# Feed-forward output projection of two layers: seven quarter products for each pair of groups in place of eight

## The chip, the cores and the metric

The kernel runs on one core of one Trainium2 chip. The metric is the device time of one execution in microseconds; the median of three runs of the kernel before is 1320.17 us (1319.09 to 1320.4). The engines are TensorE (PE: matmuls, and PEld: its weight loads), VectorE (DVE), ScalarE (ACT), GpSimd (POOL) and SyncE (SP, which issues the transfers). SBUF is the on-chip memory that all of them read; PSUM, in eight banks of 128 x 512 words, is where TensorE writes its sums, and is called a bank here.

## The reference

Two decoder layers on 512 tokens of width 1024. Each layer has an attention part, a residual sum and a normalization, and then the part that the change is in, a feed-forward of width 2816:

```python
g, u = jnp.split(x @ w_gu, 2, axis=-1)
ffn = (jax.nn.silu(g) * u) @ w_down
ple = (p_i @ w_pp) * jax.nn.sigmoid(x @ w_pg)
return layer_norm(DN_ALPHA * x + ffn + ple, ln2_g, ln2_b)
```

All numbers are float32. `w_gu` is 1024 x 5632, `w_down` 2816 x 1024.

## The kernel before

TensorE multiplies rounded numbers, so each float32 operand is kept as a high part (a cast) and a low part (the operand less its high part), and each product is three matmuls: high x high, high x low, low x high (`mm3`, lines 253 to 256). The residual rows x0 to x3 are four tiles of 128 tokens by 1024.

**Weights** pass through one queue in the order in which they are used. A tile of up to 128 x 1024 words is loaded by SyncE into one of three buffers `wst` (L209), cast by ScalarE into the high half of one of five buffers `wsp` (L234), and GpSimd subtracts to make the low half (L235, "a split" in what follows). A `wsp` buffer comes free when TensorE has done its last matmul with it; that lets the cast of the tile five places on begin.

**The feed-forward** runs over 11 groups of 256 columns in each layer. `gate_up` makes a group: four weight tiles, 96 matmuls of 512 columns, then for each half of the group (the even and the odd 128 columns) a Silu (L793), a product on VectorE (L794, which reads a bank), a cast on ScalarE (L796) and a subtraction on VectorE (L797, both of whose inputs are in SBUF). The result is the transposed activation, 128 features by 512 tokens, in two parts. `GROUPS` cuts the 11 groups in two: after groups 0 to 5, and after 6 to 10, the output projection is made for all of them. For each half of the 1024 output columns four banks (one for each 128 tokens) take up the products with all the groups' weights, 24 matmuls for a group and column half, and only then `res_out` adds each bank to its residual rows (L715 the first time, where the residual is scaled, L713 after that). So there are 16 such additions in a layer.

**The layer's start.** The rows are normalized one tile after the other on VectorE (L340 and L342, on 128 x 1024 words, all inputs in SBUF; small steps L290 to L298 between them), TensorE transposes them (L350), and ScalarE and VectorE make the two parts (L352, L353). `gate_up` of group 0 does the tokens of x0 and x1 first, then needs x2 and x3.

The order of each engine's instructions is made when the program is built, by a scheduler; the functions below set the dependences and the buffers.

Of the kernel before, what the change touches and what calls it, by code (L numbers as in the profile page):

```python
# [26 lines left out]
FF = 2816  # L27
# [60 lines left out]
def hybrid_kernel(ctx: ExitStack, tc: tile.TileContext, x, p, positions, ln_in_g, ln_in_b, w_in,  # L88
# [83 lines left out]
    GROUPS = ((0, 6), (6, FF // 256))  # L172
    for l in range(L):
        for k, a in ((0, 3), (3, 3), (6, 2)):
            plan(a, rows(w_in[l], k, a, QI, NIN))
        for k in range(0, KT, 2):
            plan(2, rows(w_in[l], k, 2, KA, KA + 256), rows(w_in[l], k, 2, KB, KB + 128))
        for c in (QA, QA + 256, QB, QB + 256):
            for k in range(0, KT, 4):
                plan(4, rows(w_in[l], k, 4, c, c + 256))  # L180
        for k0 in (0, 4):
            for h in range(2):
                for k in range(k0, k0 + 4, 2):
                    plan(2, rows(w_o[l], k, 2, h * 512, (h + 1) * 512))
        for lo, hi in GROUPS:
            for f in range(lo, hi):
# [3 lines left out]
            for h in range(2):  # L190
                for f in range(lo, hi):
                    plan(2, rows(w_down[l], 2 * f, 2, h * 512, (h + 1) * 512))
# [9 lines left out]

    def w_pump():
        while True:
            go = False
            if wpos["dma"] < len(wq) and wpos["dma"] < wpos["split"] + ST_AHEAD:
                a, cols, _ = wq[wpos["dma"]]
                n = sum(ap.shape[1] for ap in cols)
                st = wst.tile([128, 1024], F32, name="wst", tag="wst")  # L209
                sv = st[:, :a * n].rearrange("p (a n) -> p a n", a=a)  # L210
                o = 0
                for ap in cols:
                    SP.dma_start(sv[:, :, o:o + ap.shape[1]], ap.rearrange("(a p) n -> p a n", p=128))
                    o += ap.shape[1]
                wst_live[wpos["dma"]] = st
                if wpos["dma"] in X_AT:
                    load_x(X_AT[wpos["dma"]])
                wpos["dma"] += 1
                go = True
            if wpos["split"] < wpos["dma"] and (wpos["room"] or wq[wpos["split"]][2]):  # L220
                i = wpos["split"]
                a, cols, extra = wq[i]
                n = sum(ap.shape[1] for ap in cols)
                st = wst_live.pop(i)
                if extra:
                    w = [[slot()[:, :n] for _ in range(a)] for _ in range(2)]
                    for k in range(a):
                        A.copy(w[0][k], st[:, k * n:(k + 1) * n])
                        V.tensor_tensor(w[1][k], st[:, k * n:(k + 1) * n], w[0][k], OP.subtract)
                    w_live[i] = w  # L230
                else:
                    wpos["room"] -= 1
                    w = wsp.tile([128, 2, 1024], F32R, name="wsp", tag="wsp")
                    A.copy(w[:, 0, :a * n], st[:, :a * n])  # L234
                    G.tensor_tensor(w[:, 1, :a * n], st[:, :a * n], w[:, 0, :a * n], OP.subtract)  # L235
                    w = w[:, :, :a * n].rearrange("p s (a n) -> p s a n", a=a)
                    w_live[i] = [[w[:, r, k] for k in range(a)] for r in range(2)]
# [5 lines left out]
    def w_take():  # L243
        i = wpos["use"]
        wpos["use"] += 1
# [7 lines left out]
    def mm3(o, sh, sl, mh, ml, start, stop):  # L253
        PE.matmul(o, sh, mh, start=start, stop=False)  # L254
        PE.matmul(o, sh, ml, start=False, stop=False)  # L255
        PE.matmul(o, sl, mh, start=False, stop=stop)  # L256
# [192 lines left out]
    for l in range(L):  # L449
# [319 lines left out]
        def gate_up(first):  # L769
# [5 lines left out]
            for r in ((0, 256), (256, 512)) if first else ((0, 512),):  # L775
                for j in range(2):
# [14 lines left out]
            for f in range(2):  # L791
                a, b = t2k(), t2k()
                A.activation(a, ps[0, f], AF.Silu)  # L793
                V.tensor_tensor(b, ps[1, f], a, OP.mult)  # L794
                h = [slot(), slot()]
                A.copy(h[0], b)  # L796
                V.tensor_tensor(h[1], b, h[0], OP.subtract)  # L797
                hs.append(h)
            return hs

        for gi, (lo, hi) in enumerate(GROUPS):
            hs = []
            for f in range(lo, hi):
                hs += gate_up(f == 0)
                if gi == 1 and f == lo:
# [9 lines left out]
            if gi == 0:  # L815
                pin = [slot(F32), slot(F32)]
                for i in range(2):
                    SP.dma_start(pin[i].rearrange("p (t n) -> p t n", t=2),
                                 p[l, 0, i * 256:(i + 1) * 256].rearrange("(t p) n -> p t n", p=128))
            for h in range(2):  # L820
# [10 lines left out]
                for t in range(NT):  # L831
                    res_out(h, ALPHA if gi == 0 else None)(t, ps[t])
# [68 lines left out]
```

## Time and profile before

| | |
|---|---|
| median of the runs | 1320.17 us (1319.09 to 1320.4) |
| the profiled execution | 1320.5 us |
| its span, from first to last instruction | 1318.7 us |
| TensorE busy, share of the span | 1271.0 us, 96% |
| VectorE busy | 613.8 us, 47% |
| GpSimd busy | 565.1 us, 43% |
| ScalarE busy | 511.7 us, 39% |
| mean granted TensorE clock | 0.985 of full speed |

The profiled execution's own time is 1.8 us more than its span. A busy share says how long an engine had work, not whether it held up the others; that is read from the idle times of the engine that is busy nearly always, and from what ended them. A matmul's row shows some 0.39 us, but they overlap: what one costs is the distance between two starts.

### The profile page before, as it was taken

To read this page: it belongs to the slowest core of one execution; us is meant where nothing else is said; L and a number is where in the kernel's file an instruction comes from. 1 tells how busy PE (TensorE), PEld (TensorE's weight loads), DVE (VectorE), ACT (ScalarE), POOL (GpSimd) and SP (SyncE) were. 2 spreads that over 40 slices of the span, in tenths; PEclk is the share of its full clock that TensorE was granted. 3 is DMA by queue.
4 is the path that set the end of the run, shared out by engine and by line. 5 is a ranking of instruction groups with operands and counts; after the bars stand their busy time and mean duration, and the time that the engine had idled before them with its cause. 6 is when DMAs were issued, how large, how long until landed. Compare 5 with 4: busy or idle time off the path is not lost.

```text
span 1318.7 us, 17770 instructions
## 1 busy us (share of the span) xinstructions
PE 1271.0 (96%) x6752; PEld 1097.1 (83%) x6752; DVE 613.8 (47%) x1522; ACT 511.7 (39%) x1056; POOL 565.1 (43%) x377
## 2 busy tenths in 40 slices
PE   6799999999999999999997999999999999999996
PEld 5799889888888888888897998979888888888885
DVE  8899965712120022113679998674121102121166
ACT  2657765333221232313336577743222212222220
POOL 7465432354444444443055544324444444444422
PEclk9899999899999999999998999999999999999998
DMA  5133011333333333324022301104332333332221
GB/s 168 49 96 97 33 33 33 97 105 99 98 113 97 96 96 97 96 96 138 12 80 81 113 33 49 48 17 144 96 96 96 112 96 96 96 96 96 96 80 48
DMA packets 88476, 112.72 MB, mean 85 GB/s; under 512 B 4804, under 2 KB 65220, under 8 KB 88392
## 3 DMA queue, kind: packets, MB, share of 16 engines
q1 hardware_dynamic: 87720, 111.57, 27.1%
q8 instruction: 53, 0.87, 0.3%
q14 instruction: 31, 0.25, 0.1%
q10 hardware_dynamic: 672, 0.03, 0.0%
HBM read 109.49 MB, written 2.10 MB: 85 GB/s over the span
## 4 chain that ended last, share of the span: by engine, by line
PE 84%; DVE 12%; ACT 2%; issue 1%; DMA 0%; POOL 0%; DVEq 0%; SPq 0%; POOLq 0%; ACTq 0%
PE bank L254 26%; PE bank L256 26%; PE bank L255 26%; PE bank L594 2%; PE bank L638 2%; DVE t2k L414 2%; DVE m L569 1%; DVE work L570 1%; DVE t2k L412 1%; PE bank L632 1%; DVE t2k L597 1%; DVE x L342 1%; DVE work L558 1%; PE bank L424 1%; PE bank L350 1%
## 5 line engine op out<-in xcount | busy, mean ns | idle before, releaser
L235 POOL TENSOR_TENSOR wsp<-wst,wsp 128x1024 fp32r<-128x1024 f32 (+3 forms) x188 | 448.9, 2392 | 527.6 <-ACT wsp L234 527.3
L234 ACT CAST wsp<-wst 128x1024 fp32r<-128x1024 f32 (+3 forms) x188 | 194.3, 1037 | 453.7 <-PE bank L256 286.5
L255 PE MATMUL bank<-fl,wsp 128*128 128x512 f32 (+1 forms) x768 | 286.1, 373 | 1.8 <-DVE fl L353 1.8
L256 PE MATMUL bank<-fh,wsp 128*128 128x512 f32 (+1 forms) x768 | 285.9, 373 | 0.0
L254 PE MATMUL bank<-fh,wsp 128*128 128x512 f32 (+1 forms) x768 | 284.9, 374 | 1.0 <-ACT fh L352 1.0
L794 DVE TENSOR_TENSOR t2k<-bank,t2k 128x512 f32<-128x512 f32 x44 | 30.0, 692 | 356.5 <-PE bank L256 356.5
L254 PE MATMUL bank<-wsp,slot 128*128 128x512 f32 x432 | 169.0, 391 | 0.0
L255 PEld LDWEIGHTS bank<-fl,wsp 128*128 128x128 f32 x768 | 145.9, 190 | 27.3 <-DVE fl L353 2.3
L256 PE MATMUL bank<-wsp,slot 128*128 128x512 f32 x432 | 168.2, 389 | 0.0
L255 PE MATMUL bank<-wsp,slot 128*128 128x512 f32 x432 | 168.2, 389 | 0.0
L254 PE MATMUL bank<-wsp,fh 128*128 128x256 f32 (+3 forms) x512 | 166.1, 326 | 1.3 <-DVE work L558 0.4
L254 PEld LDWEIGHTS bank<-fh,wsp 128*128 128x128 f32 x768 | 144.8, 190 | 26.6 <-ACT fh L352 1.9
L256 PEld LDWEIGHTS bank<-fh,wsp 128*128 128x128 f32 x768 | 145.8, 190 | 24.9
L256 PE MATMUL bank<-wsp,fl 128*128 128x256 f32 (+3 forms) x512 | 165.0, 323 | 1.5 <-DVE fl L353 1.5
L255 PE MATMUL bank<-wsp,fh 128*128 128x256 f32 (+3 forms) x512 | 164.5, 322 | 0.0
L254 PEld LDWEIGHTS bank<-wsp,fh 128*128 128x128 f32 x512 | 98.3, 192 | 7.7 <-ACT fh L352 1.0
L256 PEld LDWEIGHTS bank<-wsp,fl 128*128 128x128 f32 x512 | 98.2, 192 | 7.0 <-DVE fl L353 2.1
L255 PEld LDWEIGHTS bank<-wsp,fh 128*128 128x128 f32 x512 | 98.6, 193 | 5.5
L256 PEld LDWEIGHTS bank<-wsp,slot 128*128 128x128 f32 x432 | 81.1, 188 | 16.9
L255 PEld LDWEIGHTS bank<-wsp,slot 128*128 128x128 f32 x432 | 81.1, 188 | 16.1
L254 PEld LDWEIGHTS bank<-wsp,slot 128*128 128x128 f32 x432 | 81.1, 188 | 16.1
L797 DVE TENSOR_TENSOR slot<-t2k,slot 128x512 fp32r<-128x512 f32 x44 | 67.7, 1576 | 19.0 <-ACT slot L796 19.0
(154 smaller groups left out, 1696.6 us busy)
## 6 DMA issues: line engine op xcount, KB each, us to landing
wst<-in_w_gu_dram SPq DMA_DIRECT2D x88, 512.0 KB, 3.4
wst<-in_w_down_dram SPq DMA_DIRECT2D x44, 512.0 KB, 3.7
wst<-in_w_in_dram SPq DMA_DIRECT2D x16, 512.0 KB, 3.6
wst<-in_w_o_dram SPq DMA_DIRECT2D x16, 512.0 KB, 3.7
wst<-in_w_pg_dram SPq DMA_DIRECT2D x16, 512.0 KB, 3.8
wst<-in_w_in_dram SPq DMA_DIRECT2D x8, 256.0 KB, 2.7
lng<-in_ln_g_dram SPq DMA_DIRECT2D x4, 512.0 KB, 4.6
lnb<-in_ln_b_dram SPq DMA_DIRECT2D x4, 512.0 KB, 4.9
```

What stands on the lines that cost most here:

```text
L234: A.copy(w[:, 0, :a * n], st[:, :a * n])
L235: G.tensor_tensor(w[:, 1, :a * n], st[:, :a * n], w[:, 0, :a * n], OP.subtract)
L254: PE.matmul(o, sh, mh, start=start, stop=False)
L255: PE.matmul(o, sh, ml, start=False, stop=False)
L256: PE.matmul(o, sl, mh, start=False, stop=stop)
L342: V.scalar_tensor_tensor(xt[t], xt[t], rs, b_t, op0=OP.mult, op1=OP.add)
L350: PE.transpose(ps[:, i * 128:(i + 1) * 128], xt[t][:, k * 128:(k + 1) * 128], idf)
L414: V.tensor_tensor(t1.rearrange("p n (u i) -> p n u i", u=2), t1.rearrange("p n (u i) -> p n u i", u=2), t2.rearrange("p n (u i) -> p n u i ...
L594: PE.matmul(ps[:, o:o + nn], qT[kind, t, g][:, j * 128:(j + 1) * 128], kT[c, s][:, k0:k0 + nn], start=(s == 0), stop=(s == 1))
L638: PE.transpose(ps[:, j * 128:(j + 1) * 128], es[j][:, b * 128:(b + 1) * 128], idf)
L794: V.tensor_tensor(b, ps[1, f], a, OP.mult)
L797: V.tensor_tensor(h[1], b, h[0], OP.subtract)
```

## The change

`GROUPS` becomes five pairs of groups and a last single one: (0, 1), (2, 3), (4, 5), (6, 7), (8, 9), (10). The output projection is made after each of them. For a pair, the left factor (512 tokens by 512 features) and the weights (512 features by 1024 columns) are cut in quarters: tokens in halves, features in even and odd chunks, columns in halves. In place of eight quarter products there are seven, of sums and differences of quarters. In what follows they are P1 to P7, in the order in which they are made; each takes 12 matmuls of 512 columns, 6 for each 128 tokens of its token half.

| product | left factor | weights | bank | then added to |
|---|---|---|---|---|
| P1 | 11 | 11 | pa | x0, x1, left columns |
| P2 | s1 | t1 | pc | x2, x3, right columns |
| P3 | 12 | 21 | pb | x0, x1, left columns |
| P4 | s2 | t2 | on top of pa | x0, x1, right columns |
| P5 | s4 | 22 | on top of pc | x0, x1, right columns |
| P6 | s3 | t3 | on top of pa | x2, x3, right columns |
| P7 | 22 | t4 | on top of pa | x2, x3, left columns |

The banks of pa and pc are read by an addition and go on being summed into. A pair needs 84 matmuls (before 96) and 14 additions to the residual rows; a layer has 78 such additions in place of 16.

The weights of a pair are loaded as eight tiles of 128 x 512 into `slot` buffers, a pair ahead. VectorE makes the sums t1 to t4 of them, eight instructions of 128 x 512 with both inputs in SBUF (in the changed kernel's numbering L243, L244 and L245 for each of the two groups, and L259 for each of them later). The seven weight operands are then cast and split in halves of 512 (L254, L255). The left factors need four sums of 256 columns for a group (L866, L867, L869, L870), and four casts and subtractions (one of 256 columns, three of 512; L855, L856) in place of two. Group 10 keeps the old way of multiplying (L796 and L797 become L855 and L856). Lines that only move: L794 is L849, L713 and L715 are L768 and L770, L235 is L275, L340 and L342 are L395 and L397, L290 to L298 are L345 to L353, and `mm3`'s L254 to L256 are L309 to L311.

The diff, cut to what matters:

```diff
-    GROUPS = ((0, 6), (6, FF // 256))
+    def plan_down(w, f):
+        wq.append(("raw", w, f))
+        for name in ("11", "t1", "21", "t2", "22", "t3", "t4"):
+            wq.append(("op", name, name == "t4"))
+
+    GROUPS = ((0, 1), (2, 3), (4, 5), (6, 7), (8, 9), (10,))
...
+    def w_dma(i):
...
+        if wq[i][0] == "raw":
+            _, w, f = wq[i]
+            for q in ("11", "12", "21", "22"):
+                h = int(q[1]) - 1
+                quarter[q] = [slot(F32) for _ in range(2)]
+                for j in range(2):
+                    r = (2 * (f + j) + int(q[0]) - 1) * 128
+                    SP.dma_start(quarter[q][j], w[r:r + 128, h * 512:(h + 1) * 512])
+            return
...
+    def w_split(i):
+        if wq[i][0] == "raw":
+            q = quarter
+            q["t1"], q["t2"] = ([t2k() for _ in range(2)] for _ in range(2))
+            for j in range(2):
+                V.tensor_tensor(q["t1"][j], q["12"][j], q["11"][j], OP.subtract)
+                V.tensor_tensor(q["t2"][j], q["22"][j], q["t1"][j], OP.subtract)
+                V.tensor_tensor(q["12"][j], q["22"][j], q["12"][j], OP.subtract)
+            q["t3"] = q.pop("12")
+            return
+        if wq[i][0] == "op":
+            src = quarter.pop(wq[i][1])
...
+            for j in range(2):
+                A.copy(w[:, 0, j], src[j])
+                G.tensor_tensor(w[:, 1, j], src[j], w[:, 0, j], OP.subtract)
+            if wq[i][1] == "11":
+                quarter["t4"] = src
+                for j in range(2):
+                    V.tensor_tensor(src[j], quarter["21"][j], quarter["t2"][j], OP.subtract)
...
+        def factors(raw):
+            lo, hi = slice(0, 256), slice(256, 512)
+            e, o = raw
+            q1, q2 = t2k(), t2k()
+            a11 = slot()
+            r = {"11": parts(e[:, lo], [a11[:, lo], a11[:, hi]])}
+            V.tensor_tensor(q1[:, lo], e[:, hi], o[:, hi], OP.add)
+            V.tensor_tensor(q1[:, hi], q1[:, lo], e[:, lo], OP.subtract)
+            s12 = parts(q1)
+            V.tensor_tensor(q2[:, lo], e[:, lo], e[:, hi], OP.subtract)
+            V.tensor_tensor(q2[:, hi], o[:, lo], q1[:, hi], OP.subtract)
+            odd, s34 = parts(o), parts(q2)
...
+            pa, pc = [acc(), acc()], [acc(), acc()]
+            w1, w5 = take(2)
+            for f in range(2):
+                product("11", w1, pa, (f,), True, True)
+                if f == 1:
+                    w_rel()
+                product("s1", w5, pc, (f,), True, True)
+            w_rel()
+            add(0, 0, pa)
+            add(1, 1, pc)
+            pb = [acc(), acc()]
+            for left, ps, new, out in (("12", pb, True, (0, 0)), ("s2", pa, False, (0, 1)),
+                                       ("s4", pc, False, (0, 1)), ("s3", pa, False, (1, 1)),
+                                       ("22", pa, False, (1, 0))):
+                w = w_take()
+                product(left, w, ps, (0, 1), new, True)
+                w_rel()
+                add(*out, ps)
```

The change moves instructions at three places. The first is VectorE in the output projection. Before, the additions of the first projection in the first layer follow its last subtractions (x0 to x3 are the residual rows, the numbered banks the sums):

```order
L797 TENSOR_TENSOR slot_4134<-t2k_4130,slot_4133 128x512
L797 TENSOR_TENSOR slot_4142<-t2k_4138,slot_4141 128x512
L715 SCALAR_TENSOR_TENSOR x0_85<-x0_85,bank_4149 128x512
L715 SCALAR_TENSOR_TENSOR x1_86<-x1_86,bank_4150 128x512
L715 SCALAR_TENSOR_TENSOR x2_87<-x2_87,bank_4151 128x512
L715 SCALAR_TENSOR_TENSOR x3_88<-x3_88,bank_4152 128x512
L715 SCALAR_TENSOR_TENSOR x0_85<-x0_85,bank_4331 128x512
L715 SCALAR_TENSOR_TENSOR x1_86<-x1_86,bank_4332 128x512
```

After, this stands there in the projection of the pair (4, 5), from the additions of pa on: the sums for the next pair (`slot` and `t2k` tiles) come between the additions.

```order
L768 TENSOR_TENSOR x0_85<-bank_4595,x0_85 128x512
L768 TENSOR_TENSOR x1_86<-bank_4596,x1_86 128x512
L768 TENSOR_TENSOR x2_87<-bank_4597,x2_87 128x512
L243 TENSOR_TENSOR t2k_4839<-slot_4767,slot_4763 128x512
L768 TENSOR_TENSOR x3_88<-bank_4598,x3_88 128x512
L768 TENSOR_TENSOR x0_85<-bank_4637,x0_85 128x512
L768 TENSOR_TENSOR x1_86<-bank_4638,x1_86 128x512
L768 TENSOR_TENSOR x0_85<-bank_4595,x0_85 128x512
L244 TENSOR_TENSOR t2k_4841<-slot_4775,t2k_4839 128x512
L245 TENSOR_TENSOR slot_4767<-slot_4775,slot_4767 128x512
L243 TENSOR_TENSOR t2k_4840<-slot_4768,slot_4764 128x512
L768 TENSOR_TENSOR x1_86<-bank_4596,x1_86 128x512
```

The second half of pa (bank_4596) is added to x1 behind four of the next pair's weight sums, and the other two sums follow after one more addition.

The second place is TensorE in the same projection. P6 is cut in its two halves (bank_4595 and bank_4596), and matmuls of the next group's gate stage (bank_4734 and bank_4735, weights wsp_4651) stand between them. Here is the end of these and the beginning of the second half:

```order
L310 MATMUL bank_4735<-fl_84,wsp_4651 128x512
L311 MATMUL bank_4735<-fh_83,wsp_4651 128x512
L309 MATMUL bank_4734<-fh_83,wsp_4651 128x512
L310 MATMUL bank_4734<-fl_84,wsp_4651 128x512
L311 MATMUL bank_4734<-fh_83,wsp_4651 128x512
L309 MATMUL bank_4596<-wsp_4617,slot_4444 128x512
L310 MATMUL bank_4596<-wsp_4617,slot_4444 128x512
L311 MATMUL bank_4596<-wsp_4617,slot_4445 128x512
```

The first matmul into bank_4596 needs the last addition of the rows above, which reads that bank. In the first pair of a layer both halves of P6 come together and the gate matmuls stand ahead of P7, and all six weight sums stand ahead of the first addition of P6; in the last pair there are none.

The third place is VectorE at the start of the first layer's feed-forward, between L340 of x3 and L342 of x2. Before:

```order
L340 SCALAR_TENSOR_TENSOR x3_88<-x3_88,lnm_3152,lng_1284 128x1024
L290 TENSOR_SCALAR lnv1_3160<-lnvar_3153 128x1
L298 TENSOR_SCALAR lns1_3091<-lnt1_3092,lns1_3091 128x1
L291 TENSOR_SCALAR lns1_3161<-lnv1_3160 128x1
L297 TENSOR_SCALAR lnt1_3092<-lns1_3091,lnv1_3090 128x1
L293 TENSOR_SCALAR lnv1_3160<-lnv1_3160 128x1
L298 TENSOR_SCALAR lns1_3091<-lnt1_3092,lns1_3091 128x1
L297 TENSOR_SCALAR lnt1_3162<-lns1_3161,lnv1_3160 128x1
L342 SCALAR_TENSOR_TENSOR x2_87<-x2_87,lns1_3091,lnb_1285 128x1024
```

After, the first pair's six sums stand there: one L243 ahead of x3's L395, an L244 and an L245 behind it, and then these rows.

```order
L352 TENSOR_SCALAR lnt1_3092<-lns1_3091,lnv1_3090 128x1
L243 TENSOR_TENSOR t2k_3435<-slot_3365,slot_3361 128x512
L346 TENSOR_SCALAR lns1_3161<-lnv1_3160 128x1
L353 TENSOR_SCALAR lns1_3091<-lnt1_3092,lns1_3091 128x1
L244 TENSOR_TENSOR t2k_3437<-slot_3373,t2k_3435 128x512
L348 TENSOR_SCALAR lnv1_3160<-lnv1_3160 128x1
L245 TENSOR_TENSOR slot_3365<-slot_3373,slot_3365 128x512
L352 TENSOR_SCALAR lnt1_3092<-lns1_3091,lnv1_3090 128x1
L352 TENSOR_SCALAR lnt1_3162<-lns1_3161,lnv1_3160 128x1
L353 TENSOR_SCALAR lns1_3091<-lnt1_3092,lns1_3091 128x1
L353 TENSOR_SCALAR lns1_3161<-lnt1_3162,lns1_3161 128x1
L397 SCALAR_TENSOR_TENSOR x2_87<-x2_87,lns1_3091,lnb_1285 128x1024
```

L397 of x2 is now behind all six sums. In the second layer the order is the same.

## Rows read from the trace of the kernel before

**Rows 1.** The page: busy time of each engine, and shares of the chain that ended last.
```profile
PE 1271.0 (96%) x6752; PEld 1097.1 (83%) x6752; DVE 613.8 (47%) x1522; ACT 511.7 (39%) x1056; POOL 565.1 (43%) x377
...
PE 84%; DVE 12%; ACT 2%; issue 1%; DMA 0%; POOL 0%; DVEq 0%; SPq 0%; POOLq 0%; ACTq 0%
```

**Rows 2.** Windows (us from:to): length, busy time of each engine (instructions), clock, DMA share, GB/s.
```profile
400.00:440.00 40.00, 40.00 (x178) 33.14 (x177) 2.73 (x4) 8.15 (x8) 17.76 (x8) 1.00 0.32 100
...
503.26:525.02 21.76, 21.76 (x97) 18.02 (x96) 4.45 (x4) 6.34 (x9) 9.56 (x4) 1.00 0.32 96
```

**Rows 3.** Timeline in an output projection, TensorE: start us, us, engine, line, operation, tiles.
```profile
400.39 0.39 PE L255 MATMUL bank<-wsp,slot 128*128 128x512 f32 x1
400.62 0.39 PE L256 MATMUL bank<-wsp,slot 128*128 128x512 f32 x1
```

**Rows 4.** Timeline around the end of one gate and up stage: VectorE, GpSimd, ScalarE, TensorE.
```profile
514.21 1.37 DVE L794 TENSOR_TENSOR t2k<-bank,t2k 128x512 f32<-128x512 f32 x2 [16.43 <-PE bank L256]
516.47 2.48 DVE L797 TENSOR_TENSOR slot<-t2k,slot 128x512 fp32r<-128x512 f32 x1 [0.89 <-ACT slot L796]
...
515.99 2.40 POOL L235 TENSOR_TENSOR wsp<-wst,wsp 128x1024 fp32r<-128x1024 f32 x1 [3.05 <-ACT wsp L234]
...
514.86 1.05 ACT L234 CAST wsp<-wst 128x1024 fp32r<-128x1024 f32 x1 [3.89 <-issue]
515.82 1.13 ACT L796 CAST slot<-t2k 128x512 fp32r<-128x512 f32 x2
...
514.62 0.39 PE L254 MATMUL bank<-fh,wsp 128*128 128x512 f32 x1
```

**Rows 5.** Source views: one line's instructions, count, ns min/median/max, first and last start, forms.
```profile
L797 DVE TENSOR_TENSOR slot<-t2k,slot x44: 677/1573/2479, 276.6 to 1203.6; 128x512 fp32r<-128x512 f32 x44
...
L794 DVE TENSOR_TENSOR t2k<-bank,t2k x44: 680/692/694, 274.7 to 1199.6; 128x512 f32<-128x512 f32 x44
...
L715 DVE SCALAR_TENSOR_TENSOR x<-x,bank x32: 656/687/689, 169.5 to 1089.8; 128x512 f32<-128x512 f32 x32
...
L342 DVE SCALAR_TENSOR_TENSOR x<-x,lns,lnb x12: 1280/1286/3158, 232.5 to 897.2; 128x1024 f32<-128x1024 f32 x12
...
L414 DVE TENSOR_TENSOR t2k<-t2k x64: 205/416/2494, 39.3 to 802.1; 128x256 f32<-128x256 f32 x32, 128x128 f32<-128x128 f32 x20, 128x64 f32<-128x64 f32 x12
...
L235 POOL TENSOR_TENSOR wsp<-wst,wsp x188: 1447/2386/3386, 9.7 to 1255.1; 128x1024 fp32r<-128x1024 f32 x174, 128x768 fp32r<-128x768 f32 x8, 128x888 fp32r<-128x888 f32 x4, 128x592 fp32r<-128x592 f32 x2
```

**Rows 6.** Timeline, start of the first layer's feed-forward: VectorE, GpSimd, TensorE.
```profile
247.59 1.99 DVE L340 SCALAR_TENSOR_TENSOR x<-x,lnm,lng 128x1024 f32<-128x1024 f32 x1
250.49 2.40 DVE L342 SCALAR_TENSOR_TENSOR x<-x,lns,lnb 128x1024 f32<-128x1024 f32 x1
...
239.59 12.21 POOL L235 TENSOR_TENSOR wsp<-wst,wsp 128x1024 fp32r<-128x1024 f32 x4 [15.92 <-ACT wsp L234]
...
254.82 1.03 PE L350 MATMUL bank<-idf,x 128*128 128x128 f32 x8
```

**Rows 7.** Timeline, start of the second layer's feed-forward: VectorE, GpSimd, TensorE.
```profile
890.55 1.99 DVE L340 SCALAR_TENSOR_TENSOR x<-x,lnm,lng 128x1024 f32<-128x1024 f32 x1
893.46 2.43 DVE L342 SCALAR_TENSOR_TENSOR x<-x,lns,lnb 128x1024 f32<-128x1024 f32 x1
...
882.55 12.26 POOL L235 TENSOR_TENSOR wsp<-wst,wsp 128x1024 fp32r<-128x1024 f32 x4 [15.91 <-ACT wsp L234]
...
895.95 1.09 PE L350 MATMUL bank<-idf,x 128*128 128x128 f32 x8 [0.38 <-DVE x L342]
```

**Rows 8.** Windows after a wait in each layer, and the TensorE rows of those waits.
```profile
246.00:252.00 6.00, 5.24 (x25) 5.17 (x25) 6.00 (x14) 2.11 (x5) 5.76 (x3) 0.50 0.58 176
...
884.00:890.00 6.00, 3.05 (x21) 2.28 (x20) 6.00 (x12) 3.80 (x9) 6.00 (x3) 1.00 0.29 87
...
244.00 1.10 PE L350 MATMUL bank<-idf,x 128*128 128x128 f32 x8 [1.71 <-DVE lns L291]
...
886.96 1.09 PE L350 MATMUL bank<-idf,x 128*128 128x128 f32 x8 [1.71 <-DVE lns L291]
```

More of the change, by code (lines that the diff above doesn't have):

```diff
@@ L189, in hybrid_kernel @@
                         plan(4, rows(w_gu[l], k, 4, c, c + 256))
[L190 to L192 removed]
+            if len(fs) == 2:
+                plan_down(w_down[l], fs[0])
+            else:
+                for h in range(2):
+                    plan(2, rows(w_down[l], 2 * fs[0], 2, h * 512, (h + 1) * 512))
         for h in range(2):
@@ L201, in hybrid_kernel @@
     wpos = dict(dma=0, split=0, use=0, room=W_AHEAD)
+    quarter = {}
+    def w_dma(i):
[10 more added lines that the diff above has]
+            return
+        a, cols, _ = wq[i]
+        n = sum(ap.shape[1] for ap in cols)
+        st = wst.tile([128, 1024], F32, name="wst", tag="wst")
+        sv = st[:, :a * n].rearrange("p (a n) -> p a n", a=a)
+        o = 0
+        for ap in cols:
+            SP.dma_start(sv[:, :, o:o + ap.shape[1]], ap.rearrange("(a p) n -> p a n", p=128))
+            o += ap.shape[1]
+        wst_live[i] = st
+        if i in X_AT:
+            load_x(X_AT[i])
@@ L205, in w_pump @@
             go = False
[L206 to L217, printed above, removed]
+            staged = sum(e[0] != "op" for e in wq[wpos["split"]:wpos["dma"]])
+            if wpos["dma"] < len(wq) and staged < ST_AHEAD:
+                w_dma(wpos["dma"])
                 wpos["dma"] += 1
                 go = True
[L220 to L237, printed above, removed]
+            i = wpos["split"]
+            if i < wpos["dma"] and (wpos["room"] or wq[i][0] == "raw" or wq[i][2] is True and wq[i][0] != "op"):
+                w_split(i)
                 wpos["split"] += 1
@@ L789, in gate_up @@
                         to_features(2 + j)
-            hs = []
[L791 to L805, printed above, removed]
+            raw = []
@@ new lines, in down, with add, product @@
+        def down(hs, first):
+            seen = set()
+            def add(half, h, ps):
+                for u in range(2):
+                    t = 2 * half + u
+                    res_out(h, ALPHA if first and (t, h) not in seen else None)(t, ps[u])
+                    seen.add((t, h))
+            def product(left, w, ps, fs, new, stop):
+                for u in range(2):
+                    c = slice(u * 128, (u + 1) * 128)
+                    for f in fs:
+                        sh, sl = hs[f][left]
+                        mm3(ps[u], sh[:, c], sl[:, c], w[0][f], w[1][f], new and f == 0, stop and f == 1, True)
+            pa, pc = [acc(), acc()], [acc(), acc()]
+            w1, w5 = take(2)
+            for f in range(2):
+                product("11", w1, pa, (f,), True, True)
[13 more added lines that the diff above has]
+                add(*out, ps)
@@ L806, in hybrid_kernel @@
+        for gi, fs in enumerate(GROUPS):
+            hs = []
+            for f in fs:
+                raw = gate_up(f == 0)
+                if len(fs) == 2:
+                    hs.append(factors(raw))
+                else:
+                    hs += [parts(a) for a in raw]
+                if gi == 1 and f == fs[0]:
                     pT = {}
```

58 lines of the change are left out of this document (50 added, 8 removed).

## The prediction

> **What bounds the kernel now.** I read the page first: TensorE is busy 1271.0 us of 1318.7 and makes up 84% of the chain that ended last, VectorE 12% [rows 1]. Then the windows, stage by stage: in the output projection (400 to 440 us) and in a gate and up stage (503.26 to 525.02) TensorE is busy in the whole stretch at a granted clock of 1.00, that is 2.4 GHz, with VectorE busy for 2.73 and 4.45 us [rows 2]. Then the timeline: matmuls of 512 columns follow each other every 0.2267 us (96 in 21.76 us, and 400.39, 400.62) [rows 2, 3]. So in the feed-forward stages a matmul removed is worth 0.2267 us, as long as TensorE never waits. What must be found is whether the added work makes it wait, and the last views look at VectorE and GpSimd together.
>
> GpSimd's split of a weight tile takes 2.4 us, and a VectorE operation whose two tensors both lie in SBUF does not run beside it: L797 is issued at 516.47 inside a split (515.99 to 518.39) and takes 2.48 us instead of 0.68, so it ends about 0.56 after the split [rows 4, 5]. It goes the other way too: the longest split took 3.386 us against a median of 2.386, the longest L342 3.158 against 1.286 [rows 5]. An operation that reads a bank does not wait: L794 stays between 680 and 694 ns, L715 between 656 and 689 [rows 5]. Before, only L797 meets this in the feed-forward, and nobody needs its result soon.
>
> The Trainium skill (SBUF — State Buffer, section "Who interferes with whom") calls this an exclusive lock: VectorE with two SBUF inputs and GpSimd block each other for whole instructions, and issue order decides who waits. The rows here agree (2.48 us against 0.68). By that rule a weight sum that is issued a moment ahead of a split would not wait; this is my first rival.
>
> **The gain.** A pair of groups needs 84 matmuls where it needed 96: 12 x 0.2267 = 2.72 us. Ten pairs (five in each layer): 27.2 us. The matmuls keep their 512 columns, and the clock there is 1.00, so I take this whole.
>
> **Work that stays hidden.** The weights are the same bytes, in eight transfers of 256 KB in place of four of 512 KB; they are issued a pair ahead, and TensorE waited for no weights before [rows 2]. GpSimd splits 14 half tiles in place of 4 whole ones. By the smallest split (1.447 us at 592 columns) and the median (2.386 at 1024), 512 columns take about 1.27, so a pair costs 17.8 us in place of 9.5, and with the eight gate and up tiles 37 of the 62.6 us that a pair takes TensorE (2 x 21.76 and 84 x 0.2267). ScalarE's casts likewise. The left factors of the pair's first group have the second group's 21.76 us as cover. Those of the second group: the products of L849 end 0.96 after the pair's first product starts (t = 0 from here; 515.58 less 514.62 in [rows 4]); five operations of 256 columns at about 0.4 (L414, at most as wide, has a median of 0.416 [rows 5]) and three of 0.68 make 4.0, and two half splits in between cost about 1.7, so all are there at 6.7. TensorE has 18 matmuls of the first group (4.08 us), then needs the "11" factors at 5.0 and the others from 6.4 to 7.7, in the order in which they come. I count nothing here; if the order slips by one half split it is 0.6 us a pair, 6 in all.
>
> **The weight sums in the middle of the projection.** VectorE also makes the next pair's six sums there, each with two SBUF tensors. At t = 6.7 it adds pa twice and pc once (0.683 each), then the first L243 waits for a half split and ends at 9.7. Four more adds follow, up to 12.43. Meanwhile GpSimd, let go by the same L243, does two half splits (2.5 us) and starts the next gate tile at 12.2, just ahead of L244. So L244, L245 and L243 now each wait for a split: tile until 14.5, L244 until 15.0; tile 17.2, L245 17.8; tile 20.0, L243 20.6. Only then comes the add of pa, second half, which ends at 21.2. TensorE: P1 to P3 until 8.16, P4 10.88, P5 13.60, 4 gate matmuls 14.51, P6 first half 15.87, 11 gate matmuls 18.36, and P6's second half waits for that add. **2.9 us lost** (21.2 less 18.36, rounded), more than the 2.72 gained. In the first pair of a layer all six sums stand ahead of the add for which P7 waits (wanted 21.8, there at 24.6): also about 2.9. The fifth pair has no next pair and no sums: 0. Four pairs in two layers: 23.2 us. Bounds: if the L244 gets in ahead of the tile, the stall is 0.6; if each of the three hand-overs costs 0.66 more, it is 4.9. I take 2.9, since sums and splits start from the same L243 (2.73 us of adds against 2.5 of splits).
>
> **The last group.** Group 10 now stands alone, and its projection follows its own gate stage. In [rows 4] the stage ends at 514.62, a weight cast (514.86, 1.05 us) stands ahead of the casts of the factors, and the first of these ends at 515.82 + 0.57 = 516.4. That was covered by the next group's matmuls; now it is a wait of about 1.9 us. Its low parts come under the 16 high matmuls. Two layers: 3.8 us.
>
> **The layer's start.** The first pair's six sums stand in the normalization of x2, ahead of L342 (L397 now). Before, x2 is ready at 250.49 + 2.40 = 252.89 and TensorE transposes it at 254.82: 1.9 us to spare [rows 6]. In the second layer it is ready at 895.89 and TensorE had been waiting 0.38 for it: nothing to spare [rows 7]. GpSimd splits four tiles back to back (239.59 to 251.80). L342 ended 1.1 after the last of them; x3's L340, at 249.58, must have waited for the third, so that ended near 248.5. The first L243 waits for it too and ends at 249.05; the fourth then runs until 251.4, and x3's L340 ends 1.1 after it, at 252.5. Five more sums (3.2) and the small steps between them (0.8) put L342 at 256.5, alone now (1.28), ready at 257.8: 4.9 late. Less 1.9 that is 3.0 in the first layer, 4.8 in the second: 7.8 us. Bounds: 3, if no sum meets a split (six sums of 0.6 less the 1.1 that L342 waited, 2.5 in each layer, less the 1.9 to spare in the first), and 9, if one of the later five meets one for another 0.6 in each layer.
>
> **Sum**, against the profiled execution's own 1320.5 us (0.3 above the median): 1320.5 - 27.2 + 23.2 + 3.8 + 7.8 = 1328.1; for the median about **1328**. With all low bounds: 1320.5 - 27.2 + 4.8 + 3.8 + 3 = 1304.9. With all high ones: 27.2 less, 39.2, 3.8 and 9 more: 1345.3.
>
> **Rivals.**
> First, the sums slip in ahead of the tiles (a stall of 0.6): 1305 to 1312. For it: VectorE misses by 0.2 us in my walk, less than its errors. Against it: three sums stand in a row, and between them a waiting split can go ahead, as L340 and L342 met one each [rows 6].
> Second, on the slow side: the clock falls in the stalls. In the first layer TensorE waited 1.71 us at 244.00, and from 246 to 252 the clock was 0.50 (1.2 GHz): 6 us at half, 3 us lost. In the second layer the same wait left it at 1.00 [rows 8]. If all eight stalls did as the first layer: 24 us, 1352; it decides the sign even where half of the waits I count are gone (17.4 us of them, and 4 x 3 of lost clock, against 27.2). The Trainium skill (TensorE: Matmul & The Clock Gate, "Part 1: The HAM clock gate") says that half clock is what an idle array falls back to; by it stalls cost more than their length, and one of two cases here shows it.
> Third, the change does what it says and nothing waits: 1293. Against it: [rows 5].
>
> **How the numbers follow.** My forecast (sums wait, clock holds, 1318 to 1342) 0.50; first rival 0.25; second 0.17, from 1340 on; third 0.05; slower through something not seen here 0.03. The range 1304 to 1349 leaves out the third and about half of the second and the last. A measurement of this kernel tells 0.2% from no change, 2.6 us. Faster by more: the first and third, 0.30. Within: the lower edge of the forecast, 0.10. Slower: 0.60. The cases lie on both sides, so beside the range stands the forecast's own, 1318 to 1342.
>
> **What the profile after would show.** Right: TensorE idle some 2 to 3 us once in each of the first four pairs of a layer, ended by a VectorE add, behind L243 to L245 of 2 us and more; 4 to 5 us of idle ahead of x2's transposes; 120 matmuls fewer at 0.2267; the adds at 0.69. Wrong: L243 to L245 at 0.68 throughout (then the first rival), a clock under 1.00 in the projections (the second), or TensorE waiting for GpSimd's half tiles or for the left factors, which I took as hidden.

## The result, and the profile after

The changed kernel takes 1327.43 us (median, 1327.04 to 1328.77); the kernel before, run beside it, 1320.29 us. The ratio is 1.0056, with a 95% interval of 1.0039 to 1.0073: slower by 7 us. The profiled execution took 1327.37 us, its span is 1325.6 (before 1320.5 and 1318.7).

First the page of the changed kernel: busy time of each engine with its number of instructions, and the shares of the chain that ended last.

```profile
PE 1255.6 (95%) x6632; PEld 1078.0 (81%) x6632; DVE 854.6 (64%) x1846; ACT 564.4 (43%) x1196; POOL 674.4 (51%) x477
...
PE 68%; DVE 24%; issue 3%; ACT 2%; POOL 1%; DMA 1%; DVEq 0%; SPq 0%; POOLq 0%; ACTq 0%
```

TensorE has 120 matmuls fewer than in [rows 1] and is busy 15.4 us less, but the span is 6.9 us longer. In the chain TensorE went from 84% to 68% and VectorE from 12% to 24%: VectorE now holds up TensorE. The timeline shows where, in four places.

**Ahead of x2's transposes.** The timeline of the first layer's start (start us, us, engine, line, operation, tiles; in brackets the idle time ahead and what ended it), for VectorE, GpSimd and TensorE, and the same TensorE row of the second layer:

```profile
246.45 2.36 DVE L243 TENSOR_TENSOR t2k<-slot 128x512 f32<-128x512 f32 x1
249.45 2.69 DVE L395 SCALAR_TENSOR_TENSOR x<-x,lnm,lng 128x1024 f32<-128x1024 f32 x1
256.23 1.28 DVE L397 SCALAR_TENSOR_TENSOR x<-x,lns,lnb 128x1024 f32<-128x1024 f32 x1
...
239.35 11.72 POOL L275 TENSOR_TENSOR wsp<-wst,wsp 128x1024 fp32r<-128x1024 f32 x4 [15.92 <-ACT wsp L274]
...
257.56 0.69 PE L405 MATMUL bank<-idf,x 128*128 128x128 f32 x2 [5.09 <-DVE x L397]
...
904.75 0.98 PE L405 MATMUL bank<-idf,x 128*128 128x128 f32 x7 [2.60 <-DVE x L397]
```

The first weight sum (L243) takes 2.36 us, L395 behind it 2.69, and L397 of x2 starts at 256.23; by the prediction's walk L243 ends at 249.05 (here 248.81) and L397 starts at 256.5. TensorE waits 5.09 and 2.60 us for x2 (before: not at all, and 0.38, [rows 6, 7]). Counted from x0's first transpose (241.25 and 884.21 before, 241.00 and 888.23 now), x2's came 13.57 and 11.74 us later before, and 16.56 and 16.52 now: 3.0 and 4.8 us more. Behind the wait in the first layer the granted clock was at half (window from:to, length, busy time of PE, PEld, DVE, ACT and POOL with their instructions, clock, DMA share, GB/s):

```profile
257.50:261.50 4.00, 3.94 (x19) 3.94 (x20) 3.38 (x8) 1.17 (x2) 0.00 (x0) 0.51 0.05 23
```

From x2's to x3's transposes it is 8.44 us in place of 6.62. That adds 1.8. In the second layer the half clock came ahead of the wait for x2:

```profile
893.00:899.60 6.60, 5.79 (x27) 5.80 (x28) 6.60 (x8) 2.09 (x5) 5.25 (x3) 0.50 0.55 167
```

TensorE was later with its work on x0 and x1 there, so it waits 2.60 us for x2 and not 5.09; x2 itself comes 16.5 us behind x0 in both layers, so this half clock costs nothing. In the kernel before it was the first layer that was at half at this place [rows 8], which fits the 1.9 us that x2 had to spare there and not in the second.

**In the first pair's projection.** VectorE's weight sums and the TensorE row that waits:

```profile
314.11 2.29 DVE L245 TENSOR_TENSOR slot<-slot 128x512 f32<-128x512 f32 x1
316.32 2.88 DVE L243 TENSOR_TENSOR t2k<-slot 128x512 f32<-128x512 f32 x1
319.72 2.30 DVE L244 TENSOR_TENSOR t2k<-slot,t2k 128x512 f32<-128x512 f32 x1
321.94 2.84 DVE L245 TENSOR_TENSOR slot<-slot 128x512 f32<-128x512 f32 x1
...
325.44 0.50 PE L309 MATMUL bank<-wsp,slot 128*128 128x512 f32 x1 [2.84 <-DVE x L768]
```

Four of the six sums take 2.3 to 2.9 us, one for each gate tile that GpSimd splits there, and TensorE is idle for 2.84. The idle time is counted from a row's end, 0.16 after the next start was due, so 3.0 us are lost. Then the clock falls:

```profile
325.40:331.40 6.00, 5.96 (x19) 4.78 (x20) 1.96 (x3) 1.05 (x1) 1.80 (x2) 0.72 0.60 176
...
326.40:329.60 3.20, 3.20 (x9) 2.45 (x8) 0.69 (x1) 0.00 (x0) 0.61 (x1) 0.50 0.71 209
```

The 0.72 is a mean of the two levels: 0.50 (1.2 GHz) in the middle, as the second row shows, and 2.4 GHz around it. Six microseconds at a mean of 0.72 lose another 1.7. The place costs 4.7 us, in both layers.

**In the three next pairs.** VectorE, GpSimd and TensorE in the projection of the pair (2, 3):

```profile
377.45 1.25 DVE L243 TENSOR_TENSOR t2k<-slot 128x512 f32<-128x512 f32 x1
378.62 2.47 DVE L768 TENSOR_TENSOR x<-bank,x 128x512 f32<-128x512 f32 x4
381.02 0.68 DVE L244 TENSOR_TENSOR t2k<-slot,t2k 128x512 f32<-128x512 f32 x1
381.62 2.89 DVE L245 TENSOR_TENSOR slot<-slot 128x512 f32<-128x512 f32 x1
384.43 2.88 DVE L243 TENSOR_TENSOR t2k<-slot 128x512 f32<-128x512 f32 x1
387.24 1.28 DVE L768 TENSOR_TENSOR x<-bank,x 128x512 f32<-128x512 f32 x2
388.44 1.67 DVE L244 TENSOR_TENSOR t2k<-slot,t2k 128x512 f32<-128x512 f32 x1
...
381.07 8.48 POOL L275 TENSOR_TENSOR wsp<-wst,wsp 128x1024 fp32r<-128x1024 f32 x3
...
387.97 0.50 PE L309 MATMUL bank<-wsp,slot 128*128 128x512 f32 x1 [0.59 <-DVE x L768]
...
391.96 0.50 PE L309 MATMUL bank<-wsp,slot 128*128 128x512 f32 x1 [0.52 <-DVE x L768]
```

Here L244 starts at 381.02 and the tile at 381.07. It takes 0.68 us, and the tile waits. Ahead of the addition for which P6's second half waits, only L245 (2.89) and L243 (2.88) wait for a tile each; behind it an L244 (1.67) does, ahead of the addition for which P7 waits. TensorE is idle twice, 0.59 us ahead of P6's second half and 0.52 ahead of P7. With the 0.16 each and a slow restart (the next starts are 0.34 away) that is 1.7 us for each of the three pairs.

**Ahead of the last group's projection.** ScalarE and TensorE:

```profile
602.67 1.04 ACT L274 CAST wsp<-wst 128x1024 fp32r<-128x1024 f32 x1 [4.39 <-PE bank L311]
603.62 1.14 ACT L855 CAST slot<-t2k 128x512 fp32r<-128x512 f32 x2
...
604.28 0.50 PE L309 MATMUL bank<-wsp,slot 128*128 128x512 f32 x1 [1.70 <-ACT slot L855]
```

The weight cast stands ahead of the factors' casts, as it did in [rows 4], and TensorE is idle for 1.70; with the 0.16 and the slow restart 2.0 us.

| | predicted | in the trace |
|---|---|---|
| 120 matmuls fewer | -27.2 | -27.2 |
| start of the two layers | 3.0 + 4.8 | 3.0 + 4.8, and 1.8 of clock |
| the first pairs' projections | 2 x 2.9 | 2 x 4.7 |
| the three next pairs | 6 x 2.9 | 6 x 1.7 |
| the last group | 2 x 1.9 | 2 x 2.0 |
| outside the feed-forward | 0 | 1.0 |
| sum | +7.6 | +7.0 |

The line "outside" is the start of the program to x0's transposes (241.25 before, 241.00 now) and the second layer's attention (230.9 and 232.1), whose TensorE instructions stand in the same order as before. The first row is the count times 0.2267 and not a reading of its own; that the sum comes within 0.1 of the 6.9 by which the spans differ speaks for it.

### The profile page after: what moved, and what is told of

The parts are those of the page before. It is cut to its first block, busy times and chain, and to the rows that moved or that the text cites. A ratio compares the mean times of both kernels' runs of the same rounds, so it can differ in the third digit from the quotient of the medians.

```text
span 1325.6 us, 18330 instructions
## 1 busy us (share of the span) xinstructions
PE 1255.6 (95%) x6632; PEld 1078.0 (81%) x6632; DVE 854.6 (64%) x1846; ACT 564.4 (43%) x1196; POOL 674.4 (51%) x477
## 4 chain that ended last, share of the span: by engine, by line
PE 68%; DVE 24%; issue 3%; ACT 2%; POOL 1%; DMA 1%; DVEq 0%; SPq 0%; POOLq 0%; ACTq 0%
PE bank L309 21%; PE bank L311 20%; PE bank L310 20%; DVE x L768 3%; DVE t2k L243 2%; DVE slot L245 2%; PE bank L649 2%; DVE t2k L469 2%; PE bank L693 2%; DVE m L624 2%; DVE work L625 2%; DVE slot L856 1%; POOL wsp L275 1%; DVE t2k L244 1%; DVE t2k L467 1%
## 5 line engine op out<-in xcount | busy, mean ns | idle before, releaser
L275 POOL TENSOR_TENSOR wsp<-wst,wsp 128x1024 fp32r<-128x1024 f32 (+2 forms) x148 | 364.7, 2478 | 270.0 <-ACT wsp L274 269.7
L309 PE MATMUL bank<-fh,wsp 128*128 128x512 f32 (+1 forms) x768 | 285.3, 374 | 1.0 <-ACT fh L407 1.0
L311 PE MATMUL bank<-fh,wsp 128*128 128x512 f32 (+1 forms) x768 | 284.9, 373 | 0.0
L274 ACT CAST wsp<-wst 128x1024 fp32r<-128x1024 f32 (+2 forms) x148 | 151.9, 1032 | 212.2 <-PE bank L311 143.2
L849 DVE TENSOR_TENSOR t2k<-bank,t2k 128x512 f32<-128x512 f32 x44 | 30.0, 691 | 284.3 <-PE bank L311 283.9
L255 POOL TENSOR_TENSOR wsp<-slot,wsp 128x512 fp32r<-128x512 f32 x100 | 135.9, 1383 | 95.6 <-ACT wsp L254 95.6
L309 PE MATMUL bank<-wsp,slot 128*128 128x512 f32 x392 | 156.7, 400 | 15.5 <-DVE x L768 12.1
L309 PEld LDWEIGHTS bank<-fh,wsp 128*128 128x128 f32 x768 | 145.3, 191 | 26.6 <-ACT fh L407 1.9
L311 PEld LDWEIGHTS bank<-fh,wsp 128*128 128x128 f32 x768 | 146.4, 191 | 25.2
L309 PE MATMUL bank<-wsp,fh 128*128 128x256 f32 (+3 forms) x512 | 166.2, 326 | 0.6 <-ACT fh L407 0.2
L311 PE MATMUL bank<-wsp,fl 128*128 128x256 f32 (+3 forms) x512 | 164.9, 323 | 1.6 <-DVE fl L408 1.6
L310 PE MATMUL bank<-wsp,slot 128*128 128x512 f32 x392 | 154.1, 393 | 0.0
L311 PE MATMUL bank<-wsp,slot 128*128 128x512 f32 x392 | 144.9, 393 | 0.0
L768 DVE TENSOR_TENSOR x<-bank,x 128x512 f32<-128x512 f32 x140 | 89.5, 681 | 40.8 <-PE bank L311 40.8
L309 PEld LDWEIGHTS bank<-wsp,fh 128*128 128x128 f32 x512 | 98.4, 193 | 7.4 <-ACT fh L407 0.9
L311 PEld LDWEIGHTS bank<-wsp,fl 128*128 128x128 f32 x512 | 98.3, 192 | 7.2 <-DVE fl L408 2.2
L309 PEld LDWEIGHTS bank<-wsp,slot 128*128 128x128 f32 x392 | 74.3, 190 | 36.6 <-DVE x L768 18.0
L254 ACT CAST wsp<-slot 128x512 fp32r<-128x512 f32 x100 | 57.1, 618 | 92.1 <-PE bank L311 56.4
```

Of the source, the lines that this page charges most:

```text
L254: A.copy(w[:, 0, j], src[j])
L255: G.tensor_tensor(w[:, 1, j], src[j], w[:, 0, j], OP.subtract)
L309: PE.matmul(o, sh, mh, start=start, stop=False, skip_group_check=again)
L310: PE.matmul(o, sh, ml, start=False, stop=False, skip_group_check=again)
L311: PE.matmul(o, sl, mh, start=False, stop=stop, skip_group_check=again)
L768: V.tensor_tensor(xt[t][:, c], ps, xt[t][:, c], OP.add)
```

## The experiments

Theory A is that of the prediction: the weight sums are put in VectorE's queue ahead of work for which TensorE waits, and each is held up there by a GpSimd instruction. In the changed kernel their durations (ns min/median/max) are:

```profile
L243 DVE TENSOR_TENSOR t2k<-slot x20: 678/1800/2884, 246.4 to 1158.4; 128x512 f32<-128x512 f32 x20
...
L244 DVE TENSOR_TENSOR t2k<-slot,t2k x20: 676/679/2296, 252.2 to 1162.4; 128x512 f32<-128x512 f32 x20
...
L245 DVE TENSOR_TENSOR slot<-slot x20: 677/1486/2891, 252.8 to 1164.0; 128x512 f32<-128x512 f32 x20
```

Uncontended one takes 0.68. The rivals: the additions on banks that are summed into again hold TensorE (R); the sums and the splits cost each other the same wherever they stand (P); the number and own time of the sums count, not GpSimd (Q).

**The sums in the gate stage of the pair's second group.** The sums of a pair are made when the second group's weights have been taken, not as soon as they are loaded:

```diff
-            if i < wpos["dma"] and (wpos["room"] or wq[i][0] == "raw" or wq[i][2] is True and wq[i][0] != "op"):
+            if i < wpos["dma"] and (wpos["room"] or wq[i][0] == "raw" or wq[i][2] is True and wq[i][0] != "op") \
+                    and (wq[i][0] != "raw" or wpos["use"] >= i):
```

> The changed kernel, but the weight sums of a pair are made only when the gate stage of its second group has begun, so that they stand between the left factors of the first group and no longer in the projection of the pair before or in the normalization of x2. Theory A (the place of the sums in VectorE's queue costs the time): the waits ahead of x2 (3.0 and 1.8 of lost clock in the first layer, 4.8 in the second) and in the projections (4.7 + 3 x 1.7 in each layer) go, 29.3 us: 1298. Rival R (the 14 additions on banks that are summed into again hold TensorE, the sums only stand beside them): only the 9.6 us at the layer's start go, 1318. Rival P (the sums and GpSimd's splits cost each other the same wherever they stand, so that the products now wait for split weights): 1310 to 1325, with TensorE's idle ended by GpSimd.

It took 1299.22 us, 0.9839 of the kernel before (0.9824 to 0.9853); A expected 1298. The sums are no longer held up, and GpSimd's half splits are:

```profile
L243 DVE TENSOR_TENSOR t2k<-slot x20: 676/679/681, 278.4 to 1163.8; 128x512 f32<-128x512 f32 x20
...
L245 DVE TENSOR_TENSOR slot<-slot x20: 673/678/681, 280.3 to 1167.2; 128x512 f32<-128x512 f32 x20
...
L255 POOL TENSOR_TENSOR wsp<-t2k,wsp x40: 1282/1293/5737, 281.5 to 1176.0; 128x512 fp32r<-128x512 f32 x40
```

The longest half split starts at 281.54 and ends at 287.27, 1.15 us after the last of a row of VectorE instructions with two SBUF inputs (286.12). In the changed kernel the longest of these took 2.53. So here GpSimd waits for VectorE, and TensorE does not wait for GpSimd. Why a row of VectorE instructions goes on here, while in the projections of the changed kernel VectorE's next sum waits for GpSimd's next tile, was not tried.

TensorE's waits for x2 and for the last group are, in the first layer:

```profile
254.50 0.76 PE L406 MATMUL bank<-idf,x 128*128 128x128 f32 x5 [0.40 <-DVE x L398]
...
589.66 0.50 PE L310 MATMUL bank<-wsp,slot 128*128 128x512 f32 x1 [1.70 <-ACT slot L856]
```

No idle time of 0.25 us or more is left in the projections of the pairs. A holds and R falls. Of P one half stands: the sums and the splits still cost each other. The other half falls: the products wait for no split weights, and the time is not 1310 to 1325.

**Without the sums.** The two loops in `w_split` that make t1 to t4 are taken out (the one for t4 is not shown in this cut):

```diff
-            for j in range(2):
-                V.tensor_tensor(q["t1"][j], q["12"][j], q["11"][j], OP.subtract)
...
+            q["t1"], q["t2"] = q["12"], q["22"]
```

> The changed kernel without the weight sums t1 to t4: the products take single quarters of the weights in their place, so the result is another. All else stands, the 14 additions of a pair and the left factors too. Theory A: 1298, as with the sums moved under the gate stage; what it is below that is what the moved sums still cost. Rival R (the additions hold TensorE): 1318.

1299.76 us, 0.9840 (0.9825 to 0.9855). So the 80 sums of the ten pairs cost nothing that can be measured once they stand under the gate stages, and the 14 additions of a pair, which are still there, hold TensorE nowhere.

**Only the first pair's sums late.**

```diff
+                    and (wq[i][0] != "raw" or wq[i][2] > 0 or wpos["use"] >= i):
```

> The changed kernel, but only the first pair's sums of each layer are made late, in the gate stage of group 1; the others stay in the projections. Theory A: the waits ahead of x2 go and nothing else, 1327.4 less 9.6: 1318, with x2's transposes 11.7 to 13.6 us after x0's as before. If x2's delay has another cause than these six sums: 1327.

1318.74 us, 0.9989 (0.9979 to 0.9999). x2's transposes come 11.8 and 13.9 us after x0's; the stalls in the projections are as in the changed kernel (2.85, then 0.56 and 0.52 three times, in both layers). The start of the layers is 9 of the 28 us, the projections the rest.

**The last group's gate stage ahead of the last pair's projection.**

```diff
+            if fs == (8, 9):
+                tail = []
+                for a in gate_up(False):
+                    tail += [parts(a)]
             if len(fs) == 2:
                 down(hs, gi == 0)
```

> The changed kernel, but the gate stage of group 10 is run ahead of the projection of the pair (8, 9), so that this projection covers the last group's Silu, product, cast and subtraction. Theory A: the 2.0 us of wait ahead of the last group's projection go in both layers, 1327.4 less 4.1: 1323.3. If that wait is not the chain from gate to first product but the last group's weights: 1327.

1326.23 us, 1.0038 (1.0025 to 1.0051): 1.2 us less than the changed kernel and not 4.1. The trace shows the forecast's 1.70 gone from both layers, and the waits in the pair (6, 7) with it, since the sums of (8, 9) came later: 3.7 us a layer. Three things took it back. TensorE waits for weights of the projection `w_pg`, behind the feed-forward, which VectorE splits and now has late:

```profile
623.64 0.50 PE L314 MATMUL bank<-slot,fh 128*128 128x512 f32 x1 [0.22 <-DVE slot L273]
```

By the distances between the starts there, that is 0.8 us in each layer. The second layer's attention took longer, 234.05 us where the changed kernel has 232.06:

```profile
654.90:888.95 234.05, 222.20 (x1473) 204.16 (x1472) 192.74 (x582) 141.06 (x380) 98.97 (x97) 0.98 0.23 66
```

```profile
656.14:888.20 232.06, 222.10 (x1473) 203.92 (x1472) 193.42 (x582) 140.28 (x380) 99.41 (x97) 0.98 0.23 67
```

There the scheduler has put TensorE's instructions in another order: by line, tiles and shape of the trace's rows, 246 of the stretch's 1472 places differ from the kernel before, and none in the changed kernel and in the runs above. That this order costs the 2 us is not shown; in the run with GpSimd's tiles in halves, below, 193 places differ and the stretch takes 231.3. And in the second layer the clock was at half behind x2's wait (x3's transposes 9.35 us after x2's, in the changed kernel 6.69). The part ahead of the first x0, with the same instructions, was 1.6 us longer in this profile, and one first pair's clock held, which gave 1.6 back. So the chain from gate to first product is the cause of the last group's wait, since the wait goes with it; the time falls by less than the forecast's 4.1 us because other places changed as well.

**Both moves together.**

> Both moves together: the weight sums in the gate stage of the pair's second group, and the gate stage of group 10 ahead of the last pair's projection. Theory A: 1299.2 less the last group's 2.0 in each layer, and the 0.85 us that TensorE then waits for the gate weights in each layer (as in the run with the last group ahead alone) comes back: 1296.8. If the last group's wait only moves: 1299.

1298.18 us (1296.68 to 1299.19), 0.9827 (0.9812 to 0.9842). It is the fastest that leaves nothing out, but it can't be told from the run with the sums late alone (0.9839), and it stands between the two expected times, 1296.8 and 1299. In its profile the wait ahead of the last group is gone from both layers. The second layer's attention takes 234.3 us, with 229 places of TensorE's order changed; in that of the sums late alone it takes 231.6.

**GpSimd's tiles in halves.**

```diff
-            G.tensor_tensor(w[:, 1, :a * n], st[:, :a * n], w[:, 0, :a * n], OP.subtract)
+            for c in (slice(0, a * n // 2), slice(a * n // 2, a * n)):
+                G.tensor_tensor(w[:, 1, c], st[:, c], w[:, 0, c], OP.subtract)
```

> The changed kernel with every weight tile's subtraction on GpSimd cut in two halves of 512 columns; VectorE's order stays as it is. Theory A says that a sum waits for the GpSimd instruction that runs, not for the tile: each wait of some 2.2 us becomes about 1.2. In the first pair four waits give back 4 us, more than the stall of 2.84, and the clock does not fall: 4.7 us a layer; in the three next pairs two waits give back 2, more than the 1.7; ahead of x2 one to two us: about 2 x 11 = 22 at best, 1307, with a half's own 0.17 us more per tile off TensorE's path: 1305 to 1313. Rival Q (the sums' own time and number hold the additions, wherever GpSimd is): 1327.

1310.15 us, 0.9919 (0.9902 to 0.9935). The sums that wait now take 1.8 us at most:

```profile
L243 DVE TENSOR_TENSOR t2k<-slot x20: 729/1476/1781, 243.4 to 1139.8; 128x512 f32<-128x512 f32 x20
...
L245 DVE TENSOR_TENSOR slot<-slot x20: 674/1774/1781, 248.7 to 1143.3; 128x512 f32<-128x512 f32 x20
```

In the pairs' projections no idle time of 0.25 us is left: as expected under A, and against Q, since the sums are as many and, in the first layer's projections, stand in VectorE's order where they stood. Ahead of x2 I expected one to two us back; nothing came: x2's transposes come 16.4 us after x0's in both layers (16.6 and 16.5 in the changed kernel). Four of the six sums there now meet a half split each. TensorE's wait is longer, as its work on x0 and x1 was done sooner:

```profile
255.39 0.90 PE L406 MATMUL bank<-idf,x 128*128 128x128 f32 x3 [6.08 <-DVE x L398]
```

The 17.3 us to the changed kernel are not the projections alone. Their stalls are 19.6; the start of the program to x0 and the second attention, whose weight tiles are halved too, give 2.8 more, x2's transposes 0.4; half clock behind x2's wait in the second layer (1.9) and behind the last group's in both (3.4) takes 5.3 back.

**GpSimd writes zeros.**

```diff
+            if a == 4 and "w_gu" in cols[0].tensor.name:
+                G.memset(w[:, 1, :a * n].bitcast(F32), 0.0)
+            else:
                 G.tensor_tensor(w[:, 1, :a * n], st[:, :a * n], w[:, 0, :a * n], OP.subtract)
```

> The changed kernel, but for the gate and up tiles GpSimd fills the low part with zeros in place of subtracting (the low part of these weights is left out, the result is another); the instruction reads nothing. VectorE's order stays. Theory A, with reads on both sides as the cause: the sums take 0.68 beside the fills, the stalls in the projections (9.8 a layer) go and x2's delay falls to the sums' own 3.6 less the 1.8 that x3's and x2's steps no longer wait: 1327.4 - 19.7 - 7.5 = 1300. If an instruction that only writes holds VectorE too, the sums wait for each fill's length, and it is between 1300 and 1327 by that length.

1296.85 us, 0.9820 (0.9806 to 0.9835); the low part of the gate and up weights is left out. Two sums and GpSimd's fill, and one sum in the projection of the pair (2, 3) with the fill beside it:

```profile
L243 DVE TENSOR_TENSOR t2k<-slot x20: 677/681/1607, 244.3 to 1126.0; 128x512 f32<-128x512 f32 x20
...
L245 DVE TENSOR_TENSOR slot<-slot x20: 674/679/686, 246.8 to 1128.4; 128x512 f32<-128x512 f32 x20
...
L276 POOL MEMSET wsp<- x88: 943/958/970, 205.9 to 1193.0; 128x1024 f32 x88
...
370.85 0.68 DVE L245 TENSOR_TENSOR slot<-slot 128x512 f32<-128x512 f32 x1
...
370.31 0.96 POOL L276 MEMSET wsp<- 128x1024 f32 x1
```

L245's 20 instructions take 0.67 to 0.69 with fills of 0.96 us in the place of the tiles. The one shown starts in the middle of a fill and is not held by it. The long L243 (eight above 1.2 us) stand beside the half splits of the pair's own weights, which still read. So in the projections a sum that is held is held by a GpSimd instruction that reads SBUF beside it, for as long as this one runs. The layers' start says nothing on that: there the last fill had ended (242.57) before the first sum began (244.29), and the scheduler had put four sums ahead of x3's normalization and not one. x2's transposes come 11.5 us after x0's in both layers, 5.0 sooner than in the changed kernel; with the half clock gone behind them that is 11.8 us where 7.5 were expected, and so the time is 3 us under the expected 1300. The Trainium skill (SBUF — State Buffer, "Who interferes with whom") says that VectorE with two SBUF inputs contends with a GpSimd instruction that reads SBUF and not with one that only writes; the two runs agree (up to 1.78 us beside half splits, 0.68 beside fills).

## Why the prediction was right, point by point

The forecast was 1328 us, slower; measured 1327.43. The mechanism was the one forecast. Three terms of the sum were sized well (the gain, the start, the last group); the stall in three of the four pairs was too large, and the clock, which the sum put at nothing, was too small.

- **The gain** of 27.2 us is there whole where nothing waits. With the sums moved, the profiled execution (1299.58) is 20.9 below that of before. The 6.3 that are missing are the last group's 4.0, x0's transposes, which come 1.5 later, and the second attention, 0.7 longer (231.6 for 230.9).
- **Work that stays hidden**: right. No TensorE wait in the pairs' projections is ended by GpSimd or by the left factors, and without the sums no such wait is left at all.
- **The start of the layers**: the walk was right to 0.3 us (L397 at 256.23 for 256.5). The half clock behind the first layer's wait, 1.8 us, was in the second rival and not in the sum.
- **The sums in the projection** is the term that was mis-sized. The walk said that L244 misses the tile by 0.2 us; it got ahead of it by 0.05. The step that failed is the price of an addition. The 0.683 came from the four L715 in 2.73 us of [rows 2], but there TensorE finishes a bank every three matmuls (3 x 0.2267 = 0.68), and the additions only keep up with it. Where the banks are ready they follow each other every 0.60: 378.62 to 381.02 for four above, and so they do in the kernel before, in the last projection of the first layer, a row that the prediction did not use:

```profile
611.94 2.47 DVE L713 TENSOR_TENSOR x<-bank,x 128x512 f32<-128x512 f32 x4
```

Over four additions that is 0.33 us, more than the 0.2 by which L244 was to miss, and it turned who goes first. So the stall is not 2.9 but 0.75 ahead of P6's second half, plus one that the walk did not follow, 0.7 ahead of P7: 1.7 in all. This is the first rival, half come true: its stall of 0.6 is near the 0.75, but the sums behind it met their tiles.
- **The first pair**: the idle time was right (3.0 for 2.9) and its price was not, 4.7. This is the second rival, come true here and behind x2's wait: the clock's mean fell to 0.72 for six us behind the 2.84 of idle, and it stayed at 1.00 behind the 0.5 of the next pairs.
- **The last group**: 1.9 forecast, 2.0 measured. Two terms were rounded up: 516.4 less 514.62 is 1.8, and 21.2 less 18.36 is 2.84; with 1.8 and 2.84 the forecast would be 0.7 lower. What it takes to get the last group's wait back was not forecast; see the run with the last group ahead.
- **The signs**: by its own list the profile was to show 2 to 3 us of idle once in each of the first four pairs. It shows that in the first pair alone; the next three have two waits of 0.5 to 0.6. The clock under 1.00 in a projection stood on the list of signs of being wrong, and it came in the first pair of both layers.
- The two mis-sizings, 7.2 us too much in the three next pairs and 5.4 too little of clock (3.6 in the first pairs, 1.8 at the start), all but cancel. The agreement of the total within 1 us is luck to that extent.

## What to carry to other kernels

An instruction that is off the critical path belongs in the queue where nobody waits behind it: the same sums cost 28 us in one place and nothing that could be measured in another, where GpSimd waited in VectorE's stead and had time for it. Before work is given to VectorE with both inputs in SBUF, look at what GpSimd runs at that moment and how long one of its instructions is; if it must stand there, cut GpSimd's instructions. And the price of an instruction in a row is its distance to the next one where nothing else sets the pace; a row in which it follows a slower engine has that engine's pace.

## What the runs showed of the hardware that was not expected

Behind one and the same wait the clock does not always do the same. The first pair's 2.83 us of idle (in the run with the last group ahead) was followed by 0.72 in the first layer and by 1.00 in the second:

```profile
326.98:332.98 6.00, 6.00 (x19) 4.77 (x20) 1.91 (x3) 1.05 (x1) 1.79 (x2) 0.72 0.57 174
974.20:980.20 6.00, 5.93 (x26) 4.93 (x27) 1.99 (x4) 1.06 (x1) 3.40 (x2) 1.00 0.57 176
```

It fell behind five of the six such waits (two in the changed kernel, two with only the first sums late, the first of these two rows) and held behind the sixth. Behind the 1.70 us ahead of the last group the clock stayed at 1.00, in both layers of the changed kernel and of the three runs that have this wait (sums late, no sums, first sums late). In the run with GpSimd's tiles in halves the like wait of 1.79 us was followed by 0.66 in both layers, and x2's wait of 6.08 by 0.67 in the first; in the run with zeros the wait of 1.79 was followed by 1.00 in the first layer and by 0.66 in the second. The first two rows are of the run with halves, the others of that with zeros:

```profile
592.45:597.45 5.00, 5.00 (x15) 4.00 (x16) 3.01 (x2) 0.47 (x1) 2.46 (x2) 0.66 0.28 69
255.40:261.40 6.00, 6.00 (x36) 6.00 (x37) 3.30 (x7) 1.17 (x2) 0.00 (x0) 0.67 0.37 115
...
588.10:593.10 5.00, 5.00 (x22) 4.15 (x23) 3.04 (x2) 0.47 (x1) 1.89 (x1) 1.00 0.30 96
...
1217.60:1222.60 5.00, 5.00 (x15) 4.00 (x16) 3.00 (x2) 0.45 (x1) 1.85 (x1) 0.66 0.36 102
```

All these figures between 0.50 and 1.00 are means over a stretch at the two levels. In these runs a wait of 1.7 to 2.9 us cost TensorE its length, or its length and some 1.7 us more, and which of them could not be told from the kernel. What decides was not tried. A time forecast from such waits is uncertain by the price of a fall for each of them (1.7 us in the projections here, 3 in [rows 8]).
